# A diffusion layer on one core: another order of the work in the first forty microseconds

## The chip, the cores and the metric

The kernel runs on one core of one Trainium2 chip. The metric is the device time of one execution in microseconds. TensorE does the matmuls, VectorE and ScalarE the elementwise work, GpSimd (POOL) a little of it, and SyncE (SP) issues nearly all loads. Each engine takes its instructions in an order that is fixed when the program is made.

## The reference

One layer: half a SwiGLU feed-forward, token mixing (attention and a long convolution), half a feed-forward. Each part is normed and modulated by rows that come from a conditioning vector. The beginning, which this case is about, is the first feed-forward on 256 latent tokens `x` and 256 context tokens `ctx`:

```python
def half_ffn(s, m, slot, g, w_up, w_down):
    h = modulate(rms_norm(s, g), chunk(m, 3 * slot), chunk(m, 3 * slot + 1))
    return s + 0.5 * chunk(m, 3 * slot + 2) * swiglu(h, w_up, w_down)

mod = (s_lat @ w_ada[l] + b_ada[l])[:, None, :]
mod_c = (s_ctx @ w_ada[l] + b_ada[l])[:, None, :]
x = half_ffn(x, mod, 0, g_norm[l, 0], w_ffn1_up[l], w_ffn1_down[l])
ctx = half_ffn(ctx, mod_c, 0, g_norm[l, 0], w_ffn1_up[l], w_ffn1_down[l])
```

The width is 2048, the inner width 5632, and everything is float32.

## The kernel before

Tokens lie along the free axis and features along the partitions, so the 2048 features are KT = 16 tiles, called d below, of 128. `xs[0]` and `xs[1]` hold latent and context tokens in eight tiles each, 256 KB a tile. A float32 matmul is made of three: a tensor is split in a rounded part (hi, on ScalarE) and a remainder (lo, on VectorE), and `mm3` multiplies hi by hi, hi by lo and lo by hi.

The work at the beginning, in the order of the program:

- The 16 loads of x (L471). For each of latent and context: squares (L480, ScalarE), their sum over eight tiles (L482, VectorE), a sum over the partitions by a matmul with ones (L487), and 1/rms in `rstd_from` (L206 to L211: one pass of VectorE, a square root on ScalarE, a reciprocal and three more passes of VectorE). The squares other than the first of a sum share two buffers (`tmp`).
- `ada_row(d)`: two loads of 1 MB each (`wrow`, L149, four buffers, so two rows) and 16 matmuls (32 instructions in the profile) that give shift and scale of feature tile d for both token sets (L153). `ada_col(d)`: a copy on ScalarE (L159), two small matmuls that turn the row into a column (L162), and four short VectorE instructions (L164, L166) that write column d of `mod`.
- `wave_h(d)`: the modulated tile d: x times scale times 1/rms (L495), hi part with the shift (L497, ScalarE), lo part (L499).
- The wave: WAVE = 3 columns j of the up-projection are computed together, for d from 0 to 15, so that the rows can be loaded meanwhile. `weight` loads a block of 512 KB for four d (L182, `raw`, four buffers), rounds it (L187, `whi`, ScalarE) and takes the remainder (L188, `wlo`, VectorE). `Ffn.tile` does the six matmuls of one d and j (L192 to L194).
- `steps`: the long convolution's filters, a generator that is advanced between the tiles (L363 to L434).

Row d + 2 and column d + 1 stand in the program ahead of tile d (`ahead = 2`). The framework's planner sets the order on each engine: it follows the program, but lets an instruction that it expects to be ready go ahead of one that it expects to wait. `tc.issue_after(ins)` adds an edge: what the block puts on the engine of `ins` comes behind `ins` there. All DMAs of SP go in one queue, in order.

After the wave, the rest of the feed-forward, the mixing and the second feed-forward follow; they are not edited.

Of the kernel before, what the change touches and what calls it, by code (L numbers as in the profile page):

```python
# [11 lines left out]
F32 = mybir.dt.float32  # L12
F32R = mybir.dt.float32r
AF = mybir.ActivationFunctionType
ALU = mybir.AluOpType
# [3 lines left out]
P = 128  # L19
D = 2048  # L20
KT = D // P
L = 256
# [7 lines left out]
WAVE = 3  # L30
# [15 lines left out]
def hybrid_layer_kernel(ctx: ExitStack, tc: tile.TileContext, a):  # L46
    nc = tc.nc
    V, S, G, PE = nc.vector, nc.scalar, nc.gpsimd, nc.tensor
# [12 lines left out]
    def U(shape, dt=F32):  # L61
        return T(up, shape, "u", dt, 58)

    def tmp(shape):
        return T(up, shape, "sq", bufs=2)
# [22 lines left out]
    sel = T(const, (P, 2), "sel")  # L88
# [18 lines left out]
    mod = [[None] * 9, [None] * 9]  # L107
# [47 lines left out]
    def ada_col(d):  # L155

        bank = ada_bank.pop(d)
        rows = tmp2((P, 2 * P))
        S.copy(rows, bank[:, 0 : 2 * P])  # L159
        col = bank[:, 2 * P : 2 * P + 4].rearrange("p (j i) -> p j i", i=2)  # L160
        for j in range(2):
            PE.matmul(col[:, j, :], rows[:, j * P : (j + 1) * P], sel, start=True, stop=True)  # L162
        for i in range(2):
            V.scalar_tensor_tensor(mod[i][1][:, d : d + 1], col[:, 0, i : i + 1], bada1[:, d : d + 1], gn[:, 0, d : d + 1],  # L164
                                   op0=ALU.add, op1=ALU.mult)
            V.tensor_add(mod[i][0][:, d : d + 1], col[:, 1, i : i + 1], bada[:, d : d + 1])  # L166


    def split(src, shape):
# [7 lines left out]
        V.tensor_sub(lo, src, hi.bitcast(F32))  # L177
        return hi, lo

    def weight(src, shape, eng=None):  # L180
        raw = T(wp, shape, "raw", bufs=4)
        load = nc.sync.dma_start(raw, src)  # L182
        if done[0]:
            last_load[0] = load
        hi = T(wp, shape, "whi", F32R, 3)
        lo = T(wp, shape, "wlo", F32R, 3)
        S.copy(hi, raw)  # L187
        (eng or V).tensor_sub(lo, raw, hi.bitcast(F32))  # L188
        return hi, lo

    def mm3(ps, w, xx, start, stop):
        PE.matmul(ps, w[0], xx[0], start=start, stop=False)  # L192
        PE.matmul(ps, w[0], xx[1], start=False, stop=False)  # L193
        PE.matmul(ps, w[1], xx[0], start=False, stop=stop)  # L194

    def mm2(ps, w, x, start, stop):

# [6 lines left out]
    def rstd_from(ss, n, shape, pool_tile, y):  # L204
        m, e = pool_tile(shape), pool_tile(shape)
        V.tensor_scalar(m, ss, 1.0 / n, EPS, op0=ALU.mult, op1=ALU.add)  # L206
        S.activation(y, m, AF.Sqrt)
        V.reciprocal(y, y)
        V.tensor_mul(e, y, y)
        V.scalar_tensor_tensor(e, e, -0.5, m, op0=ALU.mult, op1=ALU.mult)  # L210
        V.scalar_tensor_tensor(y, e, 1.5, y, op0=ALU.add, op1=ALU.mult)  # L211

    def col_rstd(*args, **kw):
        for _ in rstd_steps(*args, **kw):
# [45 lines left out]
    class Ffn:  # L260
# [17 lines left out]

        def tile(self, k, k4, w, ps2):
            for half in range(2):  # L280
                self.mm(ps2[half], (w[0][:, k4, half, :], w[1][:, k4, half, :]), self.h[k], k == 0, k == KT - 1)

        def close(self, j, ps2):
            sg = tmp2((P, 2, L))
# [182 lines left out]
    steps = filter_spectrum()  # L467
    for i in range(2):
        for q in range(KT // 2):
            t = U((P, 2, L))  # L470
# [2 lines left out]
    V.tensor_scalar(bada1, bada[:, KT : 2 * KT], 1.0, None, op0=ALU.add)  # L473
    f1 = Ffn(2, a["w_up1"], a["w_dn1"], 0)
    rs = U((P, 2, L))
    for i in range(2):
        acc = None
        for t in xs[i]:
            sq = tmp((P, 2, L)) if acc else U((P, 2, L))
            S.activation(sq, t, AF.Square)  # L480
            if acc:
                V.tensor_add(acc, acc, sq)  # L482
            else:
                acc = sq
        ps = PB((P, L))
        for j in range(2):
            PE.matmul(ps, ones, acc[:, j, :], start=j == 0, stop=j == 1)  # L487
        rstd_from(ps, D, (P, L), tmp2, rs[:, i, :])
    next(steps)

    def wave_h(d):
        hi, lo = U((P, 2, L), F32R), U((P, 2, L), F32R)
        t = T(up, (P, 2, L), "sq", bufs=2)
        for i in range(2):
            V.scalar_tensor_tensor(t[:, i, :], xd(i, d), mod[i][1][:, d : d + 1], rs[:, i, :], op0=ALU.mult, op1=ALU.mult)  # L495
        for i in range(2):
            S.activation(hi[:, i, :], t[:, i, :], AF.Identity, bias=mod[i][0][:, d : d + 1])  # L497
        for i in range(2):
            V.scalar_tensor_tensor(lo[:, i, :], t[:, i, :], mod[i][0][:, d : d + 1], hi[:, i, :].bitcast(F32),  # L499
                                   op0=ALU.add, op1=ALU.subtract)  # L500
        f1.h[d] = (hi, lo)


    wave = [f1.open(alt=j >= 2) for j in range(WAVE)]
    ahead = 2
    for e in range(ahead):
        ada_row(e)
        if e:
            ada_col(e - 1)
    w = {}  # L510
    for d in range(KT):
        if d + ahead < KT:
            ada_row(d + ahead)
        if d + ahead - 1 < KT:
            ada_col(d + ahead - 1)
        wave_h(d)
        for j in range(WAVE):
            if d % 4 == 0:
                w[j] = weight(f1.wup[j, d // 4], (P, 4, 2, P))
            f1.tile(d, d % 4, w[j], wave[j])  # L520
            if j < 2 or d < 2:
                next(steps, None)
    for _ in steps:
        pass
    for j in range(WAVE):
# [203 lines left out]
    for half in range(2):  # L729
# [31 lines left out]
        for i in range(4):  # L761
            ct = half * 4 + i
            ps = PB((P, L))
# [86 lines left out]
    y = []  # L850
# [164 lines left out]
```

## Time and profile before

| | us |
|---|---|
| median of 3 runs | 2748.61 (2746.44 to 2749.71) |
| the profiled execution | 2746.74 |
| its span | 2744.9 |
| TensorE busy in it | 2669.3 |
| VectorE, ScalarE, GpSimd busy | 1864.9, 962.5, 235.3 |

The profiled execution has its own time, to which all rows below belong; it lies 1.87 us under the median. A row of a timeline gives start, duration, engine, line, operation, tiles and count, and in brackets the idle time of the engine before it with what ended that. PE is TensorE, PEld its weight loads, DVE is VectorE, ACT is ScalarE, SPq is SyncE's queue. PEclk of 1.00 is 2.4 GHz, 0.5 is 1.2 GHz.

### The profile page before, as it was taken

What the parts mean: (1) busy time and instruction counts of PE and PEld (TensorE: products, weight loads), DVE (VectorE), ACT (ScalarE), POOL (GpSimd) and SP (SyncE); (2) the same over time, 40 slices, a digit from 0 to 9 for tenths busy, and PEclk for the clock granted to TensorE, in tenths of its full rate; (3) what the DMA queues carried; (4) which work ended last, traced back from release to release, by engine and by line L of the source; (5) the groups of instructions that cost most, each with busy time, mean ns of one, the idle gap of its engine ahead of it and who ended that gap; (6) DMA issues with size and microseconds to landing.
All of it is one profiled execution on the core that took longest, in us unless ns stands there. A gap on an engine that the chain in (4) does not pass through costs nothing. (4 is left out here: it accounts for less than half of the span.)

```text
span 2744.9 us, 35199 instructions
## 1 busy us (share of the span) xinstructions
PE 2669.3 (97%) x13494; PEld 2225.4 (81%) x13494; DVE 1864.9 (68%) x3044; ACT 962.5 (35%) x1307; POOL 235.3 (9%) x112
## 2 busy tenths in 40 slices
PE   5999999999999999999999999988999999999999
PEld 3678888888888888888888878777788888888888
DVE  5679899977686666434342897878666666666666
ACT  3343222222222222222222555355454444444443
POOL 0000000000000000000000620232101111111111
PEclk9999999999999999999999999999999999999999
DMA  9876566665686666422222355224545555555555
GB/s 347 304 250 231 209 214 234 215 228 204 228 292 229 221 211 219 158 93 100 98 95 99 132 185 187 93 92 140 173 162 185 187 185 186 185 186 185 187 186 169
DMA packets 144351, 513.47 MB, mean 187 GB/s; under 512 B 17175, under 2 KB 21432, under 8 KB 139832
## 3 DMA queue, kind: packets, MB, share of 16 engines
q1 hardware_dynamic: 139968, 506.32, 53.7%
q10 hardware_dynamic: 4216, 4.91, 0.6%
q8 instruction: 106, 1.74, 0.2%
q14 instruction: 61, 0.50, 0.1%
HBM read 506.98 MB, written 4.19 MB: 186 GB/s over the span
## 5 line engine op out<-in xcount | busy, mean ns | idle before, releaser
L187 ACT CAST whi<-raw 128x1024 fp32r<-128x1024 f32 x648 | 680.3, 1050 | 1301.6 <-PE pa L193 486.0
L188 DVE TENSOR_TENSOR wlo<-raw,whi 128x1024 fp32r<-128x1024 f32 x572 | 705.1, 1233 | 481.4 <-ACT whi L187 471.4
L200 PE MATMUL pa<-u,whi 128*128 128x512 f32 x2016 | 715.3, 401 | 10.3 <-DVE u L245 5.9
L193 PE MATMUL pa<-u,whi 128*128 128x512 f32 x1376 | 538.0, 391 | 1.5 <-DVE u L499 1.5
L192 PE MATMUL pa<-u,whi 128*128 128x512 f32 x1376 | 536.3, 391 | 1.8 <-ACT u L497 1.7
L194 PE MATMUL pa<-u,wlo 128*128 128x512 f32 x1376 | 537.8, 391 | 0.0
L202 PE MATMUL pa<-u,wlo 128*128 128x256 f32 x1890 | 533.2, 282 | 2.9 <-POOL wlo L188 1.9
L200 PEld LDWEIGHTS pa<-u,whi 128*128 128x128 f32 x2016 | 377.9, 189 | 98.2 <-issue 6.3
L188 POOL TENSOR_TENSOR wlo<-raw,whi 128x1024 fp32r<-128x1024 f32 x76 | 189.7, 2496 | 2282.5 <-ACT whi L187 2267.6
L202 PEld LDWEIGHTS pa<-u,wlo 128*128 128x128 f32 x1890 | 359.7, 190 | 7.4 <-POOL wlo L188 2.3
L192 PEld LDWEIGHTS pa<-u,whi 128*128 128x128 f32 x1376 | 258.2, 188 | 59.7 <-ACT u L497 3.8
L193 PEld LDWEIGHTS pa<-u,whi 128*128 128x128 f32 x1376 | 259.5, 189 | 56.2 <-DVE u L499 2.2
L194 PEld LDWEIGHTS pa<-u,wlo 128*128 128x128 f32 x1376 | 259.3, 189 | 55.1 <-issue 1.2
L192 PE MATMUL pb<-u,whi 128*128 128x512 f32 (+1 forms) x800 | 300.2, 376 | 2.4 <-DVE u L581 2.3
L194 PE MATMUL pb<-u,wlo 128*128 128x512 f32 (+1 forms) x800 | 299.1, 374 | 2.5 <-DVE wlo L188 2.5
L193 PE MATMUL pb<-u,whi 128*128 128x512 f32 (+1 forms) x800 | 299.0, 374 | 0.0
L200 PE MATMUL pb<-u,whi 128*128 128x512 f32 x736 | 250.4, 399 | 2.2 <-DVE u L320 2.2
L126 DVE CUSTOM_DVE_ANT_0 adas<-adaw,crow,bada 128x1024 bf16<-128x1024 f32 x160 | 205.1, 1282 | 29.3 <-DMA adaw<-in_w_adaT_dram 19.9
L126 DVE CUSTOM_DVE_ANT_0 adas<-adaw,crow,mod 128x1024 bf16<-128x1024 f32 x160 | 205.2, 1282 | 20.9 <-DMA adaw<-in_w_adaT_dram 17.9
L192 PEld LDWEIGHTS pb<-u,whi 128*128 128x128 f32 x800 | 152.4, 191 | 33.3 <-issue 4.5
L194 PEld LDWEIGHTS pb<-u,wlo 128*128 128x128 f32 x800 | 152.1, 190 | 29.0 <-DVE wlo L188 2.7
L193 PEld LDWEIGHTS pb<-u,whi 128*128 128x128 f32 x800 | 152.3, 190 | 26.4 <-issue 0.4
(199 smaller groups left out, 2288.4 us busy)
## 6 DMA issues: line engine op xcount, KB each, us to landing
raw<-in_w_up_dram SPq DMA_DIRECT2D x352, 512.0 KB, 3.6
adaw<-in_w_adaT_dram SPq DMA_DIRECT2D x223, 512.0 KB, 4.9
raw<-in_w_dn_dram SPq DMA_DIRECT2D x184, 512.0 KB, 3.5
wrow<-in_w_ada_dram SPq DMA_DIRECT2D x32, 1024.0 KB, 7.8
raw<-in_w_hy_dram SPq DMA_DIRECT2D x32, 512.0 KB, 3.5
raw<-in_w_o_dram SPq DMA_DIRECT2D x32, 512.0 KB, 3.5
raw<-in_w_kv_dram SPq DMA_DIRECT2D x16, 512.0 KB, 3.8
raw<-in_w_q_dram SPq DMA_DIRECT2D x16, 512.0 KB, 3.5
```

The lines of the kernel that those rows point to most:

```text
L126: V.tensor_tensor_reduce(out=sc, in0=t, in1=crow[i][:, b * (D // 2) : (b + 1) * (D // 2)], scale=1.0, scalar=mcol if b else bada[:, n : n ...
L187: S.copy(hi, raw)
L188: (eng or V).tensor_sub(lo, raw, hi.bitcast(F32))
L192: PE.matmul(ps, w[0], xx[0], start=start, stop=False)
L193: PE.matmul(ps, w[0], xx[1], start=False, stop=False)
L194: PE.matmul(ps, w[1], xx[0], start=False, stop=stop)
L200: PE.matmul(ps, w[0], x, start=start, stop=stop)
L202: PE.matmul(ps[:, 0, :], w[1], x[:, 0, :], start=False, stop=False)
```

## The change

- `ada_row(0)` comes before the norm sums in the program, and all squares have buffers of the large pool `U`.
- `ada_row(1)`, `ada_col(0)` and `wave_h(0)` come next, then the three first weight blocks. Their remainders (`wlo`, on VectorE) get an edge behind the last instruction of `wave_h(0)`. Their loads and rounding copies get none. `ada_col(1)` follows.
- `ada_row(2)` and the filter step of the first tile come behind the tile's matmuls, with an edge on TensorE to the last of them.
- From d = 1 on the loop is as it was. Several helpers return their last instruction; `rs_last` is not used.

```diff
-    def weight(src, shape, eng=None):
+    def weight(src, shape, eng=None, behind=None):
...
         S.copy(hi, raw)
-        (eng or V).tensor_sub(lo, raw, hi.bitcast(F32))
+        if behind is None:
+            (eng or V).tensor_sub(lo, raw, hi.bitcast(F32))
+        else:
+            with tc.issue_after(behind.ins):
+                V.tensor_sub(lo, raw, hi.bitcast(F32))
         return hi, lo
...
     rs = U((P, 2, L))
+    ada_row(0)
     for i in range(2):
         acc = None
         for t in xs[i]:
-            sq = tmp((P, 2, L)) if acc else U((P, 2, L))
+            sq = U((P, 2, L))
...
     ahead = 2
-    for e in range(ahead):
-        ada_row(e)
-        if e:
-            ada_col(e - 1)
-    w = {}
+    ada_row(1)
+    ada_col(0)
+    h_last = wave_h(0)
+    w = {j: weight(f1.wup[j, 0], (P, 4, 2, P), behind=h_last) for j in range(WAVE)}
+    ada_col(1)
     for d in range(KT):
-        if d + ahead < KT:
-            ada_row(d + ahead)
-        if d + ahead - 1 < KT:
-            ada_col(d + ahead - 1)
-        wave_h(d)
+        if d:
+            if d + ahead < KT:
+                ada_row(d + ahead)
+            if d + ahead - 1 < KT:
+                ada_col(d + ahead - 1)
+            wave_h(d)
         for j in range(WAVE):
-            if d % 4 == 0:
+            if d and d % 4 == 0:
                 w[j] = weight(f1.wup[j, d // 4], (P, 4, 2, P))
-            f1.tile(d, d % 4, w[j], wave[j])
-            if j < 2 or d < 2:
-                next(steps, None)
+            mm = f1.tile(d, d % 4, w[j], wave[j])
+            with ExitStack() as first:
+                if d == j == 0:
+                    first.enter_context(tc.issue_after(mm.ins))
+                    ada_row(ahead)
+                if j < 2 or d < 2:
+                    next(steps, None)
```

## Rows read from the trace of the kernel before

**Rows 1.** The page, first part: busy time and share of the span.
```profile
PE 2669.3 (97%) x13494; PEld 2225.4 (81%) x13494; DVE 1864.9 (68%) x3044; ACT 962.5 (35%) x1307; POOL 235.3 (9%) x112
```

**Rows 2.** Table by stretch: length, busy time (instructions) by engine, clock, DMA share, GB/s.
```profile
0.00:25.00 25.00, 4.18 (x12) 2.45 (x16) 13.67 (x25) 12.74 (x20) 0.70 (x6) 1.00 0.93 344
25.00:38.06 13.06, 7.74 (x88) 4.03 (x88) 9.24 (x22) 4.99 (x8) 0.00 (x0) 0.81 0.96 368
38.06:45.36 7.30, 7.30 (x43) 4.79 (x39) 3.07 (x9) 2.08 (x3) 0.00 (x0) 0.86 1.01 417
45.36:70.00 24.64, 19.52 (x152) 12.02 (x153) 12.88 (x43) 8.48 (x18) 0.00 (x0) 1.00 0.90 322
70.00:80.00 10.00, 10.00 (x57) 7.58 (x61) 8.61 (x19) 4.52 (x7) 0.00 (x0) 0.83 0.31 129
80.00:170.00 90.00, 89.96 (x608) 59.70 (x600) 50.32 (x128) 34.70 (x60) 0.00 (x0) 1.00 0.82 302
```

**Rows 3.** Timeline, 0 to 29 us: norm sums, 1/rms, rows 0 and 1.
```profile
6.87 5.41 DVE L482 TENSOR_TENSOR u<-u,sq 128x512 f32<-128x512 f32 x7 [1.23 <-ACT u L480]
...
14.90 0.42 ACT L207 ACTIVATE u<-sg 128x256 f32<-128x256 f32 x1 [0.24 <-DVE sg L206]
...
15.35 1.75 DVE L208 RECIPROCAL u<-u 128x256 f32<-128x256 f32 x1 [0.48 <-ACT u L207]
...
22.90 2.08 PE L487 MATMUL pb<-u,ones 128*128 128x256 f32 x4 [8.50 <-DVE u L482]
...
24.91 4.37 PE L153 MATMUL pb<-wrow,csp 128*32 128x256 f32 x64
```

**Rows 4.** Timeline, 27 to 39 us: weights, second 1/rms, first tile.
```profile
27.71 1.04 ACT L187 CAST whi<-raw 128x1024 fp32r<-128x1024 f32 x1 [5.79 <-DMA raw<-in_w_up_dram]
28.79 1.23 DVE L188 TENSOR_TENSOR wlo<-raw,whi 128x1024 fp32r<-128x1024 f32 x1 [5.94 <-ACT whi L187]
...
29.93 0.42 DVE L206 TENSOR_SCALAR sg<-pb 128x256 f32<-128x256 f32 x1
...
30.70 1.03 ACT L187 CAST whi<-raw 128x1024 fp32r<-128x1024 f32 x1
...
33.06 1.16 DVE L188 TENSOR_TENSOR wlo<-raw,whi 128x1024 fp32r<-128x1024 f32 x1
...
36.02 1.27 DVE L495 SCALAR_TENSOR_TENSOR sq<-u,mod,u 128x256 f32<-128x256 f32 x3
...
36.20 1.94 PE L153 MATMUL pb<-wrow,csp 128*32 128x256 f32 x16 [2.03 <-DMA wrow<-in_w_ada_dram]
36.54 0.91 ACT L497 ACTIVATE u<-sq,mod 128x256 fp32r<-128x256 f32 x2 [3.42 <-DVE sq L495]
...
37.21 0.88 DVE L499 SCALAR_TENSOR_TENSOR u<-sq,mod,u 128x256 fp32r<-128x256 f32 x2
...
38.07 1.22 PE L192 MATMUL pa<-u,whi 128*128 128x512 f32 x2
```

**Rows 5.** Timeline of SP's queue, 21 to 58 us: issues of loads.
```profile
21.05 9.32 SPq L182 DMA_DIRECT2D raw<-in_w_up_dram  x5
30.48 27.82 SPq L149 DMA_DIRECT2D wrow<-in_w_ada_dram  x10
```

**Rows 6.** Table by stretch: one tile (d=0, j=0), row 3, the d=1 tiles.
```profile
38.15:40.55 2.40, 2.40 (x6) 1.65 (x6) 0.33 (x1) 0.00 (x0) 0.00 (x0) 0.60 1.03 423
46.39:48.32 1.93, 1.93 (x32) 1.09 (x32) 1.83 (x6) 0.00 (x0) 0.00 (x0) 1.00 0.96 383
51.14:55.47 4.33, 4.33 (x18) 3.30 (x18) 3.56 (x11) 0.63 (x2) 0.00 (x0) 1.00 0.89 360
```

**Rows 7.** Timeline, 41 to 51 us: half of row 2, a column, a filter pair.
```profile
41.79 1.07 PE L153 MATMUL pb<-wrow,csp 128*32 128x256 f32 x16
...
48.86 0.61 PE L162 MATMUL pb<-sel,sg 128*128 128x2 f32 x4 [0.54 <-ACT sg L159]
...
50.34 0.64 PE L363 MATMUL pb<-u,u 64*64 64x256 f32 x2 [0.87 <-ACT u L372]
```

More of the change, by code (lines that the diff above doesn't have):

```diff
@@ L161, in ada_col @@
         for j in range(2):
-            PE.matmul(col[:, j, :], rows[:, j * P : (j + 1) * P], sel, start=True, stop=True)
+            last = PE.matmul(col[:, j, :], rows[:, j * P : (j + 1) * P], sel, start=True, stop=True)
         for i in range(2):
@@ L166, in ada_col @@
             V.tensor_add(mod[i][0][:, d : d + 1], col[:, 1, i : i + 1], bada[:, d : d + 1])
+        return last
     def split(src, shape):
@@ L193, in mm3 @@
         PE.matmul(ps, w[0], xx[1], start=False, stop=False)
-        PE.matmul(ps, w[1], xx[0], start=False, stop=stop)
+        return PE.matmul(ps, w[1], xx[0], start=False, stop=stop)
     def mm2(ps, w, x, start, stop):
@@ L210, in rstd_from @@
         V.scalar_tensor_tensor(e, e, -0.5, m, op0=ALU.mult, op1=ALU.mult)
-        V.scalar_tensor_tensor(y, e, 1.5, y, op0=ALU.add, op1=ALU.mult)
+        return V.scalar_tensor_tensor(y, e, 1.5, y, op0=ALU.add, op1=ALU.mult)
     def col_rstd(*args, **kw):
@@ L280, in tile @@
             for half in range(2):
-                self.mm(ps2[half], (w[0][:, k4, half, :], w[1][:, k4, half, :]), self.h[k], k == 0, k == KT - 1)
+                mm = self.mm(ps2[half], (w[0][:, k4, half, :], w[1][:, k4, half, :]), self.h[k], k == 0, k == KT - 1)
+            return mm
         def close(self, j, ps2):
@@ L487, in hybrid_layer_kernel @@
             PE.matmul(ps, ones, acc[:, j, :], start=j == 0, stop=j == 1)
-        rstd_from(ps, D, (P, L), tmp2, rs[:, i, :])
+        rs_last = rstd_from(ps, D, (P, L), tmp2, rs[:, i, :])
     next(steps)
@@ L498, in wave_h @@
         for i in range(2):
-            V.scalar_tensor_tensor(lo[:, i, :], t[:, i, :], mod[i][0][:, d : d + 1], hi[:, i, :].bitcast(F32),
-                                   op0=ALU.add, op1=ALU.subtract)
+            last = V.scalar_tensor_tensor(lo[:, i, :], t[:, i, :], mod[i][0][:, d : d + 1], hi[:, i, :].bitcast(F32),
+                                          op0=ALU.add, op1=ALU.subtract)
         f1.h[d] = (hi, lo)
+        return last
     wave = [f1.open(alt=j >= 2) for j in range(WAVE)]
     ahead = 2
-    for e in range(ahead):
-        ada_row(e)
-        if e:
-            ada_col(e - 1)
-    w = {}
-    for d in range(KT):
-        if d + ahead < KT:
-            ada_row(d + ahead)
-        if d + ahead - 1 < KT:
-            ada_col(d + ahead - 1)
-        wave_h(d)
+    ada_row(1)
[3 more added lines that the diff above has]
+    ada_col(1)
+    for d in range(KT):
+        if d:
[4 more added lines that the diff above has]
+            wave_h(d)
         for j in range(WAVE):
-            if d % 4 == 0:
+            if d and d % 4 == 0:
                 w[j] = weight(f1.wup[j, d // 4], (P, 4, 2, P))
-            f1.tile(d, d % 4, w[j], wave[j])
-            if j < 2 or d < 2:
-                next(steps, None)
+            mm = f1.tile(d, d % 4, w[j], wave[j])
[5 more added lines that the diff above has]
+                    next(steps, None)
     for _ in steps:
```

## The prediction

> **What bounds the kernel now.** I read the page first: TensorE is busy for 97% of the span [rows 1], so the whole kernel can only become shorter by the time in which TensorE waits or runs at half clock. The table by stretch [rows 2] then shows where that is near the beginning. From 80 to 170 us TensorE is busy for 89.96 of 90 us at the full clock; before that it is not: 4.18 of the first 25 us, 7.74 of the next 13.06 (clock 0.81), 19.52 of the 24.64 from 45.36 on, and a mean clock of 0.83 from 70 to 80. The change touches this stretch only. The same table shows the second resource: the DMA engines are busy 0.93 to 1.01 until 45 us and 0.90 until 70, then idle (0.31) for ten. So up to 70 us TensorE waits for chains and for bytes, after 80 it is the bound. What is gained by 80 us moves everything behind it by as much, as the rest of the program is not edited.
>
> **Why the first feed-forward matmul starts at 38.07.** The timeline of 0 to 38 us tells it [rows 3, 4]. The second norm sum leaves TensorE at 24.98 (22.90 + 2.08), but the instruction that reads it, L206, starts at 29.93. VectorE was idle; it takes its instructions in order, and ahead of L206 stood the first weight remainder (L188, wlo), which waited until 28.75 for its rounded weights (L187), and these for their load at 27.7. Two more remainders stand inside the 1/rms chain, the last at 33.06 right ahead of L209. The modulated tile (L495, L497, L499) follows at 36.02. On TensorE the first half of row 2 (L153, 1.94 us) stands ahead of it, after 2.03 us of waiting for its load.
>
> **Part 1, squares without the two-buffer limit, row 0 first.** The first sum's additions took 5.41 us for seven, 0.77 each, at the pace of squares and loads [rows 3]. In the second, VectorE also has the first 1/rms: L206 0.42, reciprocal 1.75, three more of about 0.42, so 3.4. From 12.28, when the first sum's additions end, 7 x 0.77 + 3.4 = 8.8 us give 21.1, against 22.90. The fourteen more buffers that the squares take cost nothing: 16 of x, 16 of squares and a few are in use then, of 58. Row 0's second load lands at about 21.0: SP's next issue, which waits for it, starts at 21.05 [rows 5]. With row 0 (a half of 4.37, thus 2.2 us, its first half before the landing) ahead of the sum, row 0 ends near 22.1, the sum at 22.1 + 2.08 = 24.2. With the sum first it ends at 23.2. I take 24.2.
>
> **Part 2, remainders behind the first tile.** L206 to L211 then run without remainders: 0.42 + ScalarE's square root 0.42 (14.90 [rows 3]) + 1.75 + 3 x 0.42 and hand-overs, 4.1 us: 28.3. L495 0.42 (1.27 for three) and L497 0.46 (0.91 for two) give 29.2, and the first weights are rounded at 28.75 [rows 4]: first matmul at **29.3** instead of 38.07. The remainders now wait for L499 (0.88): 30.2 + 3 x 1.23 = 33.9. Queued behind them on VectorE are column 1 and the second tile, on TensorE the matmuls with wlo of each of three tiles; the last two end at 34.5. Before, the d=0 tiles ended at 45.36, with 1.07 of row 2 and 0.64 of a filter pair between them [rows 7], so at 43.65 by the same count: 9.1 us.
>
> **Part 3, row 2 behind the first tile's matmuls.** Its first half goes from ahead of 38.07 to behind 29.3; at full clock a half row costs 1.0 (1.93 for a row [rows 6]), so 1.0 of the 9.1 is owed back: 8.1. Its loads are DMAs on SP, and the edge ties TensorE's instructions alone. The filter step in the same block costs nothing: its matmuls ran behind the first tile before, too (from 40.56, after the window of six [rows 6]).
>
> **What is late next: the loads.** In before, row 3 (46.39) stands ahead of the d=1 tiles (51.14) on TensorE [rows 6], and row 4 ahead of d=2. I assume that this order stays, as the program's order is the same. I count to the start of row 4, 55.48 in before (right after the d=1 window). Work from 29.3 to there: two sets of tiles 2 x 4.33, rows 2 and 3 2 x 1.93, two columns at 0.6, three filter matmul pairs at 0.64 [rows 6, 7]: 15.6, so 45 without a wait. But row 3 has to land. By then x (4 MiB), rows 0 to 3 (8) and four weight loads (2) must have come, with constants 14.9 MB (1e6 bytes); 344 GB/s x 25 us are 8.6 [rows 2]. The other 6.3 take 17.1 us at 368 GB/s, 15.1 at 417: 42.1 or 40.1. I take 42. In before the fifth weight load stood ahead of row 2 in SP's queue; it reuses the buffer that the first remainder frees, so row 2 was issued only at 30.48 [rows 5]. In after, row 0 is read before that remainder can start, so row 2's loads can go right behind the fourth weight load, before 28 (an estimate: without the last wait in those 9.32 us). TensorE would be ready for row 3 at 37.7 (34.5, row 2, a column, a filter pair), waits, ends it at 43, then column 3, d=1 and a filter pair, 5.6: 48.6. That is 55.48 - 48.6 = **6.9 us** earlier. What follows (waits of 5.1 us from 45.36 to 70, less than full clock from 70 to 80 [rows 2]) I leave as it is, for 0: the loads and chains behind it move with their issue.
>
> The Trainium skill, "DMA: Bandwidth & Descriptors", Specifications, puts the limit of a core's HBM traffic at about 358 GB/s. This trace moved 417 over 7.3 us [rows 2], so the measurement decides; by 358, the 6.3 MB would take 17.6 us, an estimate from that page, and the sum would be 6.3.
>
> **Sum.** The profiled execution took 2746.74, 1.84 beyond its span of 2744.9; the median is 2748.61, 1.87 above it. 2746.74 - 6.9 + 1.87 = **2741.7**. Later stages have TensorE nearly full, so nothing there takes the gain back that the rows show; their order may differ by some hundred ns either way.
>
> **Rivals.**
> 1. *The d=1 tiles go ahead of row 3.* For it: the second half of row 2 already sits between the d=0 tiles, so the order is not strictly the program's. Against it: row 3 stands ahead of its tiles as a whole (46.39, 51.14). Nothing waits for loads then: 55.48 - 45 = 10.5 us, so 2738.1. Chance 0.2.
> 2. *The loads come no earlier.* Row 3 lands at 45.9 as before (used at 46.39). Against it: SP's issue at 30.48. Then 6.9 - 3.9 = 3.0 us, 2745.6. Chance 0.22.
> 3. *The square root waits behind the weights.* The rounding copies have no edge and ScalarE is in order too. Two of the three copies stand ahead of the second square root in before. Behind one, the chain starts anew at 28.75 and d=0 ends at 38.3; behind all three (30.70 + 1.03 = 31.7) at 41.3. The first is nearly hidden by row 3's load, the second leaves rows 2 and 3, a column and 5.6 us: 51.4, 4.1 us gained, 2744.5. Chance 0.1.
> The Trainium skill, "TensorE: Matmul & The Clock Gate", What's actually happening, says that TensorE is throttled by default and activity releases it. The trace agrees (0.60 from 38.15 to 40.55, after the waits [rows 6]). If the waits for rows 2 and 3 throttle it again, d=1's 18 matmuls cost 0.40 instead of 0.24 each, 2.9 us, and 6.9 becomes 4.0; this lies inside the range.
> 4. *Slower: SP's queue keeps the fifth weight load ahead of row 2.* That load waits for the first remainder, which now ends later than 30.0. Every us later makes rows 2 and 3 a us later with idle DMAs, starting from rival 2's 3.0; it decides the sign from a remainder that ends after 33.0. With the square root behind all three copies it ends at 38.2: 8.2 later, -5.2, and half clock after the wait 2.9 more: 2756.7. Against it: row 0 is read before the first tile exists, so row 2's buffers are free before the remainder is even allowed to start. Chance 0.06.
>
> **How the numbers follow.** The forecast has 0.42. About 0.2% (5.5 us) is what a measurement of this kernel can tell from no change. Faster by that: forecast and rival 1, 0.62. Within it: rivals 2 and 3, 0.32. Slower: 0.06. The range goes from 2736 (rival 1 with 2 of the 5.1 us of waits gone) to 2747 (rival 2 with another us or two lost). The likeliest case alone spans 2739.5 (row 3 at 40.1) to 2743.
>
> **What would show it.** Right: L206 of the second sum starts within 0.5 us of its matmuls; first feed-forward matmul at 29 to 30; SP issues row 2 before 28; row 4's matmuls start at 48 to 49. Wrong: a first matmul after 33 (rival 3), row 3 still waiting past 45 (rival 2), row 2's issue after 31 (rival 4), or waits of TensorE between 80 and 170 us that before has not.

## The result, and the profile after

The changed kernel takes 2750.14 us (median of 22 executions, 2748.45 to 2754.14), the kernel before, run on the same chip between them, 2745.55 (22 executions, 2742.86 to 2750.45). The ratio is 1.0018, 95% interval 1.0012 to 1.0025: slower by 4.6 us, where 6.9 us less were predicted, and above the range (2747). The median of three that the prediction added to, 2748.61, is 3.1 us above that of the 22. The profiled execution took 2750.02, with a span of 2748.2 against 2744.9.

The table by stretch of the changed kernel answers to [rows 2], with the same columns:

```profile
0.00:25.00 25.00, 5.20 (x36) 2.38 (x36) 8.33 (x16) 9.58 (x16) 0.70 (x6) 1.00 0.94 350
25.00:38.06 13.06, 6.82 (x44) 3.64 (x44) 9.39 (x20) 6.34 (x11) 0.00 (x0) 0.61 0.86 325
38.06:45.36 7.30, 6.14 (x43) 3.91 (x44) 5.94 (x13) 0.98 (x3) 0.00 (x0) 0.77 0.49 190
45.36:70.00 24.64, 21.54 (x140) 13.28 (x142) 12.83 (x43) 7.60 (x14) 0.00 (x0) 0.93 0.90 340
70.00:80.00 10.00, 8.10 (x47) 5.58 (x38) 6.82 (x16) 6.25 (x11) 0.00 (x0) 0.83 0.90 344
80.00:170.00 90.00, 90.00 (x625) 60.07 (x624) 54.46 (x137) 32.09 (x57) 0.00 (x0) 1.00 0.78 281
```

Behind 80 us nothing has changed: 90.00 of 90 us busy. The loss lies ahead of it: half as many TensorE instructions from 25 to 38 us (44 against 88) at a clock of 0.61, and from 38 to 45 DMA engines at 0.49, where they were at 1.01. The rest follows as it did: from the end of the 288th tile matmul (the last of the 16 x 18 of this wave) to the end of the span it is 2563.4 us, in the kernel before 2562.9.

The timeline of TensorE up to 40 us tells why (columns as in [rows 3]: start, busy, engine, line, count, and in brackets the idle time ahead and what ended it):

```profile
18.26 1.94 PE L153 MATMUL pb<-wrow,csp 128*32 128x256 f32 x16 [18.26 <-DMA wrow<-in_w_ada_dram]
20.13 2.07 PE L494 MATMUL pb<-u,ones 128*128 128x256 f32 x4
22.13 1.33 PE L153 MATMUL pb<-wrow,csp 128*32 128x256 f32 x16
30.70 2.07 PE L494 MATMUL pb<-u,ones 128*128 128x256 f32 x4 [7.23 <-DVE u L489]
32.70 3.64 PE L153 MATMUL pb<-wrow,csp 128*32 128x256 f32 x32
36.27 0.64 PE L162 MATMUL pb<-sel,sg 128*128 128x2 f32 x4
37.42 0.61 PE L162 MATMUL pb<-sel,sg 128*128 128x2 f32 x4 [0.52 <-ACT sg L159]
39.22 1.18 PE L197 MATMUL pa<-u,whi 128*128 128x512 f32 x3 [1.19 <-ACT u L504]
```

TensorE's first instruction is now row 0, which waits for its load until 18.26. Behind it stands the **first** norm sum, whose squares were added up at 11.9: it starts at 20.13 instead of 12.33. The second sum starts at 30.70 instead of 22.90 [rows 3], later by the same 7.8. ScalarE's timeline, 9 to 41 us, and VectorE's:

```profile
22.70 0.42 ACT L212 ACTIVATE u<-sg 128x256 f32<-128x256 f32 x1 [10.49 <-DVE sg L211]
...
23.02 0.61 ACT L487 ACTIVATE u<-u 128x512 f32<-128x512 f32 x1
...
38.26 0.91 ACT L504 ACTIVATE u<-sq,mod 128x256 fp32r<-128x256 f32 x2 [0.89 <-DVE sq L502]
```
```profile
22.24 0.42 DVE L211 TENSOR_SCALAR sg<-pb 128x256 f32<-128x256 f32 x1 [10.34 <-PE pb L494]
...
27.56 3.08 DVE L489 TENSOR_TENSOR u<-u,u 128x512 f32<-128x512 f32 x4
32.80 0.42 DVE L211 TENSOR_SCALAR sg<-pb 128x256 f32<-128x256 f32 x1 [2.17 <-PE pb L494]
...
37.02 0.22 DVE L164 SCALAR_TENSOR_TENSOR mod<-pb,bada,gn 128x1 f32<-128x1 f32 x1 [0.64 <-PE pb L162]
...
37.75 0.87 DVE L502 SCALAR_TENSOR_TENSOR sq<-u,mod,u 128x256 f32<-128x256 f32 x2
```

ScalarE stands idle for 10.49 us at the first square root (L212), and the whole second set of squares (L487) stands behind that root, from 23.02. So the late first sum makes the second one late. What the change was to do for the second 1/rms it does: L211 follows its sum at once (32.77, 32.80), and from the end of the sum to the first tile it is 6.45 us, before 13.1 (24.98 to 38.07). The two together give the first tile: 7.8 later and 6.6 less behind it, 39.22 against 38.07 [rows 4].

One row of SP's queue, 9 to 45 us, shows rows 2 to 4 being loaded:

```profile
26.99 17.76 SPq L149 DMA_DIRECT2D wrow<-in_w_ada_dram  x5
```

Row 2 is issued at 26.99, 3.5 us earlier than before [rows 5]. Row 3's loads take row 1's buffers and are issued at 34.69 and 36.40, when row 1 has been read; row 4's take row 2's, which TensorE reads from 43.29, behind the first tile's matmuls, and the last issue of this group is at 44.42. That is why the DMA engines run dry from 38 to 45 us. Yet nobody waits for these bytes: row 3 has landed at 42.41 and is used at 50.52, row 4's first half has landed at 49.15 and is used from 55.73.

TensorE's timeline, 50 to 64 us, shows rows 3 and 4 being used:

```profile
50.52 3.35 PE L153 MATMUL pb<-wrow,csp 128*32 128x256 f32 x32
...
55.73 0.59 PE L153 MATMUL pb<-wrow,csp 128*32 128x256 f32 x2
...
60.59 1.93 PE L153 MATMUL pb<-wrow,csp 128*32 128x256 f32 x30
```

Row 3 runs at half clock for the most part (3.35 us, before 1.93 [rows 6]). Only two of row 4's 32 instructions stand ahead of the d=1 tiles, thirty stand behind them, at 60.59; before, all 32 start at 55.48, behind d=1. So the changed kernel is 1.1 us late at the first tile, 2.5 at the end of d=0 (47.83 against 45.36) and 5.1 at the end of d=1 (60.66 against 55.55).

### The profile page after: what moved, and what is told of

It is laid out like the page before. It is cut to its first block, busy times and chain, and to the rows that moved or that the text cites. A ratio compares the mean times of both kernels' runs of the same rounds, so it can differ in the third digit from the quotient of the medians.

```text
span 2748.2 us, 35191 instructions
## 1 busy us (share of the span) xinstructions
PE 2671.5 (97%) x13494; PEld 2225.2 (81%) x13494; DVE 1865.8 (68%) x3044; ACT 962.0 (35%) x1307; POOL 235.4 (9%) x112
## 5 line engine op out<-in xcount | busy, mean ns | idle before, releaser
L188 ACT CAST whi<-raw 128x1024 fp32r<-128x1024 f32 x648 | 680.9, 1051 | 1297.5 <-PE pa L198 481.7
L126 DVE CUSTOM_DVE_ANT_0 adas<-adaw,crow,bada 128x1024 bf16<-128x1024 f32 x160 | 205.0, 1282 | 29.3 <-DMA adaw<-in_w_adaT_dram 20.0
L126 DVE CUSTOM_DVE_ANT_0 adas<-adaw,crow,mod 128x1024 bf16<-128x1024 f32 x160 | 205.2, 1282 | 16.3 <-DMA adaw<-in_w_adaT_dram 13.1
```

The lines of the kernel that those rows point to most:

```text
L126: V.tensor_tensor_reduce(out=sc, in0=t, in1=crow[i][:, b * (D // 2) : (b + 1) * (D // 2)], scale=1.0, scalar=mcol if b else bada[:, n : n ...
```

## The experiments

Two theories at first. **A**: row 0's place ahead of the first sum costs what the change gains. **B**: the remainders that are held back cost it. The table has every kernel by starts in its trace: the two sums, the first feed-forward matmul (first tile), the 55th (first of d=3), and the end of the 288th. A ratio is that of the times to the kernel before, run beside it, with its 95% interval; the other columns are one profiled execution each, and the executions of one kernel lie up to some 10 us apart. The profiled ones of n4, p1 and p3 are the slowest of their kernel, that of t2 is the fastest. The kernels n undo or make parts of the change, p move the filters, q and r1 try other orders, r2 to r4 load fewer bytes, t fill TensorE's idle time.

| kernel | sums | first tile | d=3 | 288th ends | ratio |
|---|---|---|---|---|---|
| before | 12.33, 22.90 | 38.07 | 69.83 | 182.01 | |
| changed | 20.13, 30.70 | 39.22 | 74.25 | 184.78 | 1.0018 (1.0012 to 1.0025) |
| n1 | 11.85, 22.41 | 35.93 | 70.23 | 180.87 | 1.0007 (0.9998 to 1.0016) |
| n2 | 11.85, 22.42 | 32.36 | 67.53 | 179.89 | 0.9996 (0.9987 to 1.0005) |
| n3 | 20.47, 31.04 | 39.41 | 73.17 | 183.20 | 1.0007 (0.9999 to 1.0016) |
| n4 | 20.45, 31.02 | 41.21 | 71.64 | 183.92 | 1.0002 (0.9993 to 1.0011) |
| p1 | 11.85, 22.41 | 32.44 | 65.88 | 178.59 | 0.9998 (0.9989 to 1.0006) |
| p2 | 12.19, 22.75 | 37.84 | 63.56 | 176.01 | 1.0015 (1.0006 to 1.0024) |
| p3 | 19.93, 30.49 | 38.95 | 68.79 | 189.32 | 1.0034 (1.0020 to 1.0047) |
| p4 | 13.79, 18.51 | 30.01 | 58.74 | 171.00 | 0.9990 (0.9982 to 0.9999) |
| q1 | 13.43, 18.15 | 29.75 | 66.18 | 177.83 | 0.9996 (0.9987 to 1.0004) |
| q2 | 20.41, 30.65 | 40.22 | 72.24 | 183.63 | 1.0011 (1.0002 to 1.0020) |
| q3 | 12.24, 22.81 | 37.22 | 72.34 | 182.08 | 1.0003 (0.9994 to 1.0012) |
| r1 | 11.76, 22.33 | 35.32 | 72.60 | 183.67 | 1.0010 (1.0001 to 1.0020) |
| r2 | 12.51, 23.08 | 37.54 | 68.18 | 176.28 | one execution |
| r3 | 13.38, 18.10 | 29.62 | 63.29 | 171.37 | one execution |
| r4 | 19.87, 30.44 | 38.89 | 72.80 | 180.84 | one execution |
| t1 | 20.34, 30.88 | 39.12 | 74.40 | 185.07 | 1.0023 (1.0014 to 1.0032) |
| t2 | 13.56, 18.29 | 29.75 | 65.50 | 175.09 | 0.9997 (0.9989 to 1.0006) |
| t3 | 20.92, 31.48 | 38.33 | 75.57 | 188.80 | 1.0025 (1.0011 to 1.0039) |

**n1_row0_behind_sums.** The changed kernel with row 0 behind both sums:

```diff
-    ada_row(0)
     for i in range(2):
...
+    ada_row(0)
     ada_row(1)
     ada_col(0)
```

> The changed kernel with one thing undone: row 0 stands behind both norm sums in the program, as before; squares in the large pool, remainders behind the first tile and row 2 behind its matmuls stay. Theory A (what costs is row 0's place: TensorE waits for row 0's load at 18 us with the first norm sum queued behind it, and the second set's squares stand behind the first square root on ScalarE): first sum at about 12 us, second sum at 21 to 23 instead of 30.7; the three rounding copies then stand ahead of the second square root, so the first feed-forward matmul comes at 35 to 37 and the time is 1 to 4 us below the kernel before. Theory B (what costs is the remainders held back behind the first tile, and row 2 and column 1 behind them): still 2 us or more above the kernel before.

The sums are 8.3 us earlier and the first tile 3.3. Why not 8? ScalarE's timeline of this kernel, 9 to 38 us:

```profile
27.00 1.04 ACT L188 CAST whi<-raw 128x1024 fp32r<-128x1024 f32 x1 [8.01 <-DMA raw<-in_w_up_dram]
...
28.54 2.14 ACT L188 CAST whi<-raw 128x1024 fp32r<-128x1024 f32 x2 [0.49 <-DMA raw<-in_w_up_dram]
...
30.59 0.41 ACT L212 ACTIVATE u<-sg 128x256 f32<-128x256 f32 x1
```

VectorE has the root's input ready at 24.95, but the three rounding copies (L188) stand ahead of the root, and wait for loads: it starts at 30.59. This is the prediction's rival 3 with all three copies. Theory A holds for the sums and the first tile; the time is not the 1 to 4 us below the kernel before that it expected, and is not resolved from that of either kernel.

**n2_copies_behind_root.** n1 with an edge that puts the copies behind the second 1/rms:

```diff
-        S.copy(hi, raw)
...
+            with tc.issue_after(behind[0].ins):
+                S.copy(hi, raw)
...
-... behind=h_last) for j in range(WAVE)}
+... behind=(rs_last, h_last)) for j in range(WAVE)}
```

> As n1, and the three rounding copies get an edge on ScalarE behind the second square root (the remainders' edge stays). Theory A with rival 3 of the prediction as the second brake: the second 1/rms is ready near 27 to 28, first feed-forward matmul at 31 to 33, time 5 to 8 us below the kernel before. Theory B: above the kernel before, as the remainders still end behind the first tile. If the loads of rows 2 and 3 are the limit by then (the prediction's term), row 3's matmuls start at 41 to 43 and the gain is about 5.

First tile 32.36. Its ratio's interval ends below the changed kernel's: with row 0 behind the sums and the copies held back, the loss is gone. But of 5.7 us at the first tile 2.3 are left at d=3, and the time is that of the kernel before, not 5 to 8 us less.

**n3_remainders_free.** The changed kernel with `behind=h_last` taken out, so that the remainders are free again:

> The changed kernel without the edge of the remainders (Part 2 undone, row 0 still ahead of the sums). Theory A: no better than the changed kernel, 2749 to 2753, since the second sum still comes at 30.7 and three remainders fall into the chain again. Theory B: back at the kernel before or under it, 2744 to 2746.

Sums and first tile as in the changed kernel (39.41 against 39.22), d=3 1.1 earlier. Theory B finds nothing in the front; the median, 2746.80, lies between the two expected ranges, and the intervals of the two ratios overlap.

**n4_row0_first_alone.** The kernel before with `ada_row(0)` ahead of the sums and nothing else:

> The kernel before with one thing done: row 0 ahead of the norm sums in the program, nothing else of the change. Theory A: first sum at 20 instead of 12.3, second sum at 29 to 31, first feed-forward matmul at 41 or later, 3 to 8 us above the kernel before. Theory B: within 2 us of the kernel before.

```profile
20.45 2.08 PE L488 MATMUL pb<-u,ones 128*128 128x256 f32 x4
...
22.45 1.93 PE L153 MATMUL pb<-wrow,csp 128*32 128x256 f32 x16
...
31.02 2.08 PE L488 MATMUL pb<-u,ones 128*128 128x256 f32 x4 [6.63 <-DVE u L483]
```

TensorE, 9 to 38 us: row 0 ahead of the first sum (20.45), its second half ahead of the second. This edit alone makes both sums 8.1 us later and the first tile 3.1. At d=3 1.8 of it is left, and in the time (1.0002) none can be seen: the sums came as theory A had them, the time as theory B.

**p1, p2, p3 (filters later).** In n2 a filter matmul waits 1.68 us for its load. These three take the filter's steps out of d=2 and d=3, so that its loads compete with fewer rows: in n2, in the kernel before, and in the changed kernel.

```diff
-                if j < 2 or d < 2:
+                if d < 2 or (d >= 4 and j < 2):
```

> n2 (row 0 behind the sums, copies behind the second root, remainders behind the first tile) with the filter steps of the d=2 and d=3 tiles left to later tiles; all steps still run. Theory A2: in n2 the front was up to 8 us early at row 4, and gave 6 of it back between d=2 and d=3, where TensorE and ScalarE, in order, waited for the filters' first loads, which came behind the rows on busy DMA engines. Then d=3 starts at 60 or before (n2: 67.5), half clock at 59 to 63 goes, and the time is 6 to 10 us below the kernel before. Rival: the loads of rows and weights are the limit themselves; then the wait moves to rows 5 and 6, and the time stays within 2 us of n2.

> The kernel before with the filter steps of d=2 and d=3 left to later tiles, nothing else. Theory A2: the same stall is in the kernel before (1 us for the load, 1.6 for d=3's hi part, 1.7 of half clock around 72): d=3 starts at 63 to 65 instead of 69.8, with filter work of about 3 us moved behind it; 2 to 5 us below the kernel before. Rival: within 1 us of the kernel before.

> The changed kernel with the filter steps of d=2 and d=3 left to later tiles. Theory A and A2: the front stays late (second sum at 30.7, first feed-forward matmul at 39.2), but the second stall goes: d=3 at 66 to 68 instead of 74.3, time 3 to 6 us below the changed kernel, about that of the kernel before. If the front's loss is really at the loads, not at the sums, nothing is gained.

d=3 comes earlier in all three (1.7, 6.3 and 5.5 us), and nothing is gained: the same filter matmuls follow later. From the end of the 288th tile matmul to the end it is 2568.4 to 2568.9 us instead of some 2563 to 2565, p2 is slower than the kernel before, and the expected gains of 2 to 10 us came in none. In p3 the wait for the filter's load is larger in its new place (0.17 us in the changed kernel):

```profile
83.83 2.04 PE L406 MATMUL pb<-u,u 64*128 64x512 f32 x2 [6.80 <-DMA u<-in_flt_w_dram]
```

The pause moves work; as a remedy it fails. So d=3 and the 288th matmul are to be compared only among kernels without it.

**p4_squares_first** (with the pause) and **q1_squares_first** (without). n2, with the first square root behind the second set's squares, which stand in a loop of their own ahead of the sums, and the second and third rounding copy behind the first tile's hi part:

```diff
+        with tc.issue_after(sq_last.ins):
+            rs_last = rstd_from(ps, D, (P, L), tmp2, rs[:, i, :])
...
+... behind=(f1.last_hi if j else rs_last, h_last)) for j in range(WAVE)}
```

> p1 and two edges more on ScalarE: the first square root behind the second set's squares, and the second and third rounding copy behind the first tile's hi part. Theory A: the second sum comes at 18 to 20 instead of 22.4, first feed-forward matmul at 29 to 30, where the first weights' load is the limit; another 1 to 3 us below p1. Rival: as row 3's load is the limit (41 to 42 us), the same as p1 within 1 us.

> The changed kernel, with row 0 behind the two norm sums again; on ScalarE the second set's squares stand ahead of the first square root, the first weight's rounding copy behind the second square root, the other two behind the first tile's hi part. All filter matmuls stay where the change has them. Theory A (row 0's place costs the front; once the chain to the first tile has nothing ahead of it on any engine, the first feed-forward matmul comes at about 30, and the rest is bytes): sums at 13.8 and 18.5, first feed-forward matmul 30.0, row 3 at 42, row 4 at 47, d=3 tiles at 64 to 66, 288th tile matmul ending at 177 to 179, 3 to 5 us earlier than in the kernel before, ratio 0.9985 +- 0.0007. Rival (the bytes give all of the front back, wherever the front starts): d=3 tiles at 67 to 70 as in n2_copies_behind_root, 288th at 180 to 182, ratio 0.9995 to 1.0005.

TensorE and ScalarE in q1 (timelines of 9 to 38 and 9 to 32 us):

```profile
13.43 2.07 PE L496 MATMUL pb<-u,ones 128*128 128x256 f32 x4 [13.43 <-DVE u L493]
...
18.15 2.08 PE L496 MATMUL pb<-u,ones 128*128 128x256 f32 x4 [2.65 <-DVE u L493]
```
```profile
17.56 0.42 ACT L214 ACTIVATE u<-sg 128x256 f32<-128x256 f32 x1
...
20.72 0.42 ACT L214 ACTIVATE u<-sg 128x256 f32<-128x256 f32 x1 [2.75 <-DVE sg L213]
...
27.36 1.04 ACT L193 CAST whi<-raw 128x1024 fp32r<-128x1024 f32 x1 [4.12 <-DMA raw<-in_w_up_dram]
```

With the squares ahead of the root the second sum follows the first by 4.7 us; in every kernel with the root ahead of them it is 10.2 to 10.6. The first tile comes at 29.75, close behind the landing of the first weight (27.36). But d=3 is at 66.18, only 3.6 us ahead of the kernel before, the 288th matmul ends 4.2 earlier, and the ratio is 0.9996: the starts are those of theory A, the ratio is that of its rival. p4 is the one kernel whose interval ends below 1, at 0.9999.

**q2_row2_ahead_again** (the changed kernel with row 2 ahead of the first tile's matmuls, as before) and **q3_row2_behind_alone** (the kernel before with row 2 behind them):

> The changed kernel with row 2 ahead of the first tile's matmuls on TensorE again, as in the kernel before; row 0 stays first and the remainders stay behind. Theory A: the delay stems from row 0's place, so sums at 20.1 and 30.7 as in the changed kernel; first feed-forward matmul 1 to 2 us later (40 to 41.5), since row 2, landed by 35.3, fills the wait ahead of it; row 4's loads are issued up to 5 us earlier; d=3 tiles at 71 to 74, 288th tile matmul ending at 183 to 185, ratio 1.0005 to 1.002. Rival C (row 2 behind the first tile is what makes the change slower, since row 2's buffers come free late and the DMA engines idle from 38 to 45): DMA share from 38 to 45 us back to 0.9 or more, d=3 tiles at 70 or earlier, ratio 1.0000 to 1.0005.

> The kernel before with one part of the change alone: row 2's matmuls behind the first tile's. Sums at 12.3 and 22.9 as before. Theory A (this part costs nothing by itself): first feed-forward matmul 1 to 2 us earlier (36 to 37), row 3 within 1 us of 46.4, d=3 tiles within 1.5 us of 69.8, ratio 0.9993 to 1.0007. Rival C (row 2 behind the first tile delays the loads of row 4): row 4's loads issued 2 us or more later than before, d=3 tiles at 71.5 or later, ratio 1.001 to 1.002.

q2: first tile 1.0 us later than in the changed kernel, the DMA share from 38 to 45 us at 0.98 again, d=3 2.0 us earlier. q3: first tile 0.85 earlier than before, d=3 2.5 later, though its 288th matmul ends as before. Row 4's loads are issued at 36.83 and 38.76 in q2, 7 us ahead of the changed kernel's (44.42, 45.28), so rival C's mechanism is there, and q3's d=3 is as late as it expected; but TensorE waits for row 4's load in neither, and no ratio resolves this part. In q3 the 2.5 us at d=3 are half clock: 10.0 us of it from the first tile to d=3, before 2.0.

**r1_row0_between_sums.** Row 0 between the two sums, where the prediction had it:

```diff
-    ada_row(0)
     for i in range(2):
...
+        if i == 0:
+            ada_row(0)
```

> The changed kernel with row 0 between the two norm sums on TensorE, where the prediction took it to be. Theory A: first sum at 11.9, second at 22.5 to 24.2, so 6 to 8 us earlier than in the changed kernel; but the three rounding copies stand ahead of the second square root on ScalarE, so the first feed-forward matmul comes at 35.5 to 37.5 and not at the 29.3 of the prediction; 288th tile matmul at 180 to 182.5; ratio 0.9995 to 1.001. Rival (the prediction's step 2 was right once row 0 is between the sums): first feed-forward matmul at 29 to 31, ratio below 0.999.

TensorE and ScalarE, 9 to 38 us:

```profile
17.60 1.94 PE L153 MATMUL pb<-wrow,csp 128*32 128x256 f32 x16 [3.77 <-DMA wrow<-in_w_ada_dram]
...
20.04 1.55 PE L153 MATMUL pb<-wrow,csp 128*32 128x256 f32 x16 [0.50 <-DMA wrow<-in_w_ada_dram]
...
22.33 1.13 PE L493 MATMUL pb<-u,ones 128*128 128x256 f32 x4 [0.74 <-DVE u L488]
...
28.06 2.13 ACT L188 CAST whi<-raw 128x1024 fp32r<-128x1024 f32 x2 [0.55 <-DMA raw<-in_w_up_dram]
...
30.10 0.41 ACT L212 ACTIVATE u<-sg 128x256 f32<-128x256 f32 x1
...
35.32 1.65 PE L197 MATMUL pa<-u,whi 128*128 128x512 f32 x3 [1.97 <-ACT u L505]
```

Row 0 fits into the gap between the sums, as predicted, and the second sum ends at 23.5 (predicted 24.2). The first tile still comes at 35.32 and not at 29.3, as the root stands behind the copies. So the prediction would have failed at a second step, had the first held.

**r2_before_half_rows, r3_q1_half_rows, r4_after_half_rows.** Why do the leads shrink behind the first tile? Here the rows from row 3 on read half their bytes, with all matmuls, in the kernel before, q1 and the changed kernel:

```diff
-            t = T(rowp, (P, 8, 2 * P), "wrow")
-            nc.sync.dma_start(t, a["w_ada1"][d, kh])
+            if d < 3 or kh == 0:
+                t = T(rowp, (P, 8, 2 * P), "wrow")
+                nc.sync.dma_start(t, a["w_ada1"][d, kh])
```

> The kernel before with half the bytes of each row from row 3 on: only the first of a row's two loads is made, and the second half's matmuls read the same buffer. All matmuls are still there; some 4 MB less come in between 30 and 70 us. Theory A (bytes are the brake behind the first tile): first feed-forward matmul at 38.1 as before, d=3 tiles at 65 to 67 instead of 69.8. Rival (order and chains are the brake): d=3 tiles at 69 to 70.

> The kernel of q1_squares_first with the same halving of the rows' bytes from row 3 on. Theory A: first feed-forward matmul 30, d=3 tiles at 57 to 60, 6 to 9 us ahead of r2_before_half_rows, so nearly the whole lead of the first tile (8.3 us) is kept, where with all bytes 3.6 of it was. Rival: the lead at d=3 stays at 3 to 5 us.

> The changed kernel with the same halving of the rows' bytes from row 3 on. Theory A: first feed-forward matmul 39.2, d=3 tiles at 66 to 68.5, within 2 us of r2_before_half_rows, so only the later first tile is left of the 4.4 us by which the changed kernel trails at d=3. Rival (its order costs by itself, row 2 behind the first tile above all): 4 us or more behind r2_before_half_rows.

The stretch from 45.36 to 70 us in r2 and r3 (first its own length, then PE, PEld, DVE, ACT, POOL, clock, DMA share, GB/s):

```profile
45.36:70.00 24.64, 20.86 (x155) 13.26 (x155) 14.29 (x45) 9.46 (x20) 0.00 (x0) 1.00 0.70 250
```
```profile
45.36:70.00 24.64, 22.51 (x140) 15.39 (x140) 15.04 (x38) 11.55 (x20) 0.00 (x0) 1.00 0.73 263
```

The DMA engines have air now (0.70, 0.73; with all bytes 0.90, 0.92), but d=3 comes only 1.4 to 2.9 us earlier. From 30 to 70 us 0.9 to 1.8 MB fewer were moved, not the 4 expected (the kernel before 351 GB/s, r2 305). q1's lead over the kernel before at d=3 is 4.9 us instead of 3.6, the changed kernel's lag 4.6 instead of 4.4. So the loads are not what takes the lead back, in the main; the 1.2 us by which q1's lead grows come from one execution each and are not resolved. Further on bytes do cost time: the 288th matmul ends 5.7, 6.5 and 3.9 us earlier than with all bytes, but q1's lead (4.9) and the changed kernel's lag (4.6) are no smaller there either.

What then does? TensorE's instructions from the first tile to d=3, summed from the trace (us; matmuls in brackets; half clock is the time in this stretch at 1.2 GHz):

| | length | idle | rows | tiles | half clock |
|---|---|---|---|---|---|
| before | 31.76 | 5.12 | 6.73 (112) | 14.66 (54) | 1.99 |
| changed | 35.03 | 5.00 | 9.52 (128) | 15.04 (54) | 7.16 |
| n1 | 34.30 | 5.67 | 8.21 (128) | 15.10 (54) | 3.58 |
| n3 | 33.77 | 2.69 | 9.28 (128) | 16.55 (54) | 9.21 |
| q1 | 36.43 | 5.54 | 8.84 (128) | 16.18 (54) | 9.12 |
| t2 | 35.75 | 5.55 | 7.96 (128) | 16.52 (54) | 6.83 |
| t3 | 37.23 | 3.23 | 10.40 (128) | 17.55 (54) | 16.46 |

In the changed kernel and in q1 TensorE does not wait much longer than before. It does half a row more (16 matmuls, 1.07 us [rows 7], which stood ahead of the first tile before), and the rest of the 3.3 and 4.7 us is about what the same work costs at half clock: 5.2 and 7.1 us more of it, which at half speed cost 2.6 and 3.6 (an estimate: half of the time). Theory **D**: half clock after idle time takes the lead back. n3 does not fit it: 2.1 us more at half clock than the changed kernel, yet 1.3 us shorter, as TensorE is idle for 2.3 us less. So half clock can stand in the place of waiting, and its sum alone does not give what an order loses.

**t1_after_filled, t3_after_filled_more, t2_q1_filled.** Matmuls whose results are overwritten fill TensorE's idle time ahead of the first tile: six and fourteen in the changed kernel ahead of the second sum, two in q1 around row 1's second half. In t1 and t3 row 1 also gets an edge behind the second sum, where it stands in the changed kernel anyway.

```diff
+        for _ in range(6 * i):
+            PE.matmul(ps, ones, xs[0][0][:, 0, :], start=True, stop=True)
         for j in range(2):
```

> The changed kernel with six more matmuls of the size of half a norm sum (1.04 us each) behind row 0 and ahead of the second norm sum, where TensorE is idle from 23.46 to 30.70; they write the bank that the sum then overwrites. Theory D (the half clock after idle time eats the gain): the stretch of half clock at 26.13 (10.24 us) is gone, row 1 takes 2.0 us instead of 3.64, first feed-forward matmul at 37.7 to 38.6, half clock from there to d=3 3.4 us or less instead of 7.2, d=3 tiles at 70.5 to 73 (74.25 in the changed kernel), 288th tile matmul at 181.5 to 183.5, ratio 1.0005 to 1.0015. Rival (the clock only accompanies it: the same time comes back as waits for loads and chains): d=3 tiles at 73.5 to 74.5, ratio 1.0015 to 1.0025.

> The kernel of q1_squares_first with two such matmuls in TensorE's idle time ahead of the first tile (one between the halves of row 1, 24.25 to 25.84, one between the first two columns, 27.44 to 28.73). Theory D: the half clock at 28.46 (6.83 us) is gone or 3.4 us, first feed-forward matmul at 29.7 to 30.3, d=0's 18 matmuls end at 36.5 to 37.5 instead of 38.77, d=3 tiles at 63.5 to 65 (66.18 in q1), 288th tile matmul at 175 to 177, ratio 0.998 to 0.9993. Rival: the loads of rows 2 and 3 take it back, d=3 tiles at 65.7 to 66.7, ratio 0.9994 to 1.0.

> The kernel of t1_after_filled with fourteen of these matmuls instead of six: at the 0.48 us each that t1 showed they take 6.7 of the 7.2 us in which TensorE is idle ahead of the second norm sum. Theory D (the half clock is what the changed kernel pays for): no half clock between 24 and 36 us, row 1 in 2.0 to 2.2 us instead of 3.64, the first feed-forward matmul at 37.5 to 38.7, half clock from there to d=3 under 4 us, d=3 tiles at 71.5 to 73, ratio 1.001 to 1.002 (t1: 1.0023). Rival (what is late is chains and order, and the clock goes down again at the next wait): first feed-forward matmul at 37.5 to 39, d=3 tiles at 73.5 to 74.5, ratio 1.0018 to 1.0028.

In t1 the six took 2.86 us instead of the 6.2 expected. Half clock began at 29.06 instead of 26.13, and the first tile (39.12) and d=3 (74.40) came as in the changed kernel; it tells little. In t3 the filling did its work (TensorE, 22 to 48 us, then two stretches):

```profile
24.47 6.31 PE L494 MATMUL pb<-u,ones 128*128 128x256 f32 x28
31.48 1.13 PE L496 MATMUL pb<-u,ones 128*128 128x256 f32 x4 [0.70 <-DVE u L489]
32.54 1.93 PE L153 MATMUL pb<-wrow,csp 128*32 128x256 f32 x32
...
38.33 1.65 PE L197 MATMUL pa<-u,whi 128*128 128x512 f32 x3 [2.20 <-ACT u L506]
```
```profile
25.00:38.06 13.06, 9.92 (x71) 7.41 (x69) 10.97 (x26) 7.83 (x14) 0.00 (x0) 0.99 1.00 380
38.06:45.36 7.30, 7.03 (x42) 4.30 (x42) 5.05 (x8) 0.22 (x1) 0.00 (x0) 0.55 0.31 130
```

Row 1 takes 1.93 us instead of 3.64, at 2.4 GHz. The Trainium skill, "TensorE: Matmul & The Clock Gate", What's actually happening, calls the throttled state the default, which activity releases; this row agrees. But the first tile still waits for its chain, now for 2.20 us, and there the clock falls (0.55 from 38 to 45): the half clock has moved from the waiting time into the tiles. d=3 is later than in the changed kernel and than either theory expected, with 16.46 us at half clock up to there, and the ratio (1.0025) shows no gain. In t2 the half clock of d=0 is gone, its 18 matmuls end at 36.86 instead of 38.77; at d=3 0.7 of the 1.9 us is left, as the clock falls again at 45.9 and 59.6. The ratio (0.9997) is no better than q1's (0.9996), though the profiled execution, the fastest of its twelve, ended 5.9 us sooner. So taking half clock away in one place did not keep a gain. D adds up for the changed kernel and q1, not for n3, and as a remedy it fails; that half clock takes the lead back is not shown by an experiment.

## Why the prediction was wrong

**What bounds the kernel: right.** The program behind 80 us moves as a whole: 2.8 us at the end of the 288th matmul, 3.3 in the span, 4.6 in the medians.

**Part 1: the step that failed.** The prediction put row 0 ahead of the second sum only, and took the first as unchanged at 12.28. In the program text the call stands ahead of the loop over both. The price could have been worked out: row 0's second load lands at about 21 [rows 5], its first at 18.1, which the trace of before shows as well (18.50), and TensorE, in order, could start the first sum not before 18.3 + 1.9 = 20.2: 7.9 us late, 7.8 measured. n4 shows that this edit alone does it, n1 that its undoing brings the sums back. A second term of this part was wrong too: the squares without their two buffers were to bring the second sum's data from 22.90 to 21.1. From sum to sum it is 10.57 us in both kernels. VectorE takes 8.40 us for the first 1/rms and the seven additions (22.24 to 30.64), near the 8.8 of the sum, but they begin when the first sum has left TensorE (at 14.44 in the kernel before), not at 12.28: the second set's squares stand behind the first root on ScalarE, and more buffers do not change that (q1: 4.7 us). That r1's second sum ends at 23.5, near the 24.2, is luck: its data came at 22.3 and not at 21.1, and it took 1.13 us instead of 2.08.

**Part 2: mechanism right, size off.** The second 1/rms does start at its sum's end. Up to the first tile it is 6.45 us, not the 5.1 of the sum (24.2 to 29.3): L502 and L504 each come as a pair, 0.87 and 0.91, where one half of each was counted, and L164 waits 0.64 us for column 0, which stands behind row 1 on TensorE. With row 0 where it was assumed (r1), the rounding copies ahead of the root would have kept the first tile at 35.3: rival 3, given 0.1, priced with the copies ending at 31.7 (30.2 in r1, 30.7 in n1). Its price for the end of d=0, 41.3, was too low for r1's 45.26, which ran at half clock.

**Part 3: right in size, not free.** Half a row (1.07 us for 1.0) went behind the first tile. That it holds back row 4's loads was not counted (DMA share 0.49 from 38 to 45 us, in q2 0.98); it did no harm that could be measured.

**The loads: right, but not the bound.** Row 2 was issued at 26.99 (before 28), row 3 landed at 42.41 (42 predicted). With the first tile at 39.22 TensorE had no use for it yet: d=0 ended at 47.83, row 3 started at 50.52, and row 4, predicted for 48.6, had two instructions at 55.73 and the other thirty at 60.59. The order that the prediction assumed held for row 3, not for all of row 4.

**From the first tile to row 4: sized without the clock.** The prediction counted its gain at the start of row 4. q1 is another kernel, but its first tile came when the prediction had it for the change (29.75), so it shows what the rest of the count was worth. Its TensorE, 41 to 58 us:

```profile
42.95 3.18 PE L153 MATMUL pb<-wrow,csp 128*32 128x256 f32 x32
...
51.57 1.94 PE L153 MATMUL pb<-wrow,csp 128*32 128x256 f32 x32
```

d=0 ended at 38.77 and not at 34.5, with half clock from 28.46 to 35.29. Row 3, whose load was in at 41.23, started at 42.95, behind a filter pair that had waited 1.12 us for ScalarE, and took 3.18 us, most of it at half clock; it was done at 46.1 and not at 43. Row 4 started at 51.57, 3.9 us earlier than in the kernel before and not 6.9. From there on the lead stayed in this trace (3.6 at d=3, 4.2 at the 288th matmul), but the ratio, 0.9996 (0.9987 to 1.0004), shows no gain. The prediction's clause on half clock behind the waits makes 4.0 of the 6.9. That is near the 3.9, but it has the half clock on the d=1 tiles, where q1 has it on d=0 and row 3; and it stood beside the sum, not in it.

**The sign.** Rival 4 gave slower 0.06, by SP's queue, which did not happen. No rival asked what stands behind row 0 on TensorE.

**Open.** How the 0.18% splits among the parts: row 0 first alone is 1.0002, with the remainders held back (q2) 1.0011, with row 2 behind as well 1.0018, and row 2 behind alone 1.0003; each interval is about 0.001 to either side. And what decides in which wait the clock falls, and why a lead of 3.9 us at row 4 (q1) is none in the time.

## What to carry to other kernels

Where an instruction is moved ahead on an engine that runs in order, write down when its own data land, and beside it when each instruction that it passes is ready: the difference is the price, and it goes on through every chain that starts there. Then follow that chain through the queues of the other engines (here the squares and the rounding copies on ScalarE); an order that frees one engine helps only as far as the next queue. A lead at one place is not a gain: count it again at the end of the stage, with the work that moved behind the place and with the time at half clock.

## What the runs showed of the hardware

Equal f32 matmul instructions (128x256, one set of weights) took 0.23 us each when twenty-eight followed each other (6.31 us in t3), and 0.52 in a sum behind idle time (2.07 for four); the sum right behind the twenty-eight took 1.13. In the first 25 us the granted clock is shown as 1.00 in all these kernels, but row 0's first half takes 1.94 us there, as half a row does in the kernel before at 36.20 [rows 4], where the record has 1.2 GHz (33.23 to 40.06), and behind a sum half a row takes 1.07 in t1 (22.32): the durations of the first instructions are those of 1.2 GHz, whatever the record shows.

Half the bytes of each row from row 3 on (r2 to r4) moved d=3 by 1.4 to 2.9 us, though in the kernel before the DMA engines were busy for 0.90 of the stretch from 45 to 70 us; here a high DMA share did not say that bytes were the main brake up to d=3. Over 7.3 us one core moved 413 GB/s again (n2, 38.06 to 45.36).
